# Half of the row sums of w_ada moved off TensorE, and another opening

## The chip, the cores and the metric

The kernel runs on one core of a Trainium2 chip. The metric is the time of one execution in microseconds (us) as the device reports it. A profiled execution gives, for every instruction, when it began and ended on its engine. The engines are TensorE (PE in the profile; PEld is its weight load), VectorE (DVE), ScalarE (ACT), GpSimd (POOL) and SyncE (SP, which here only issues DMAs). SBUF is the memory on the chip that all of them read, PSUM the one into which TensorE writes its products.

## What is computed

One decoder layer for a sequence of 1024 tokens, width 2048, in float32:

```python
mod = silu(c) @ W_ada + b_ada            # c: (1, 2048), W_ada: (2048, 6144)
shift, scale, gate = split(mod, 3)
h = rms_norm(x, norm_gain) * (1 + scale) + shift
proj = h @ w_in                          # w_in: (2048, 8192)
...                                      # stick-breaking attention and chunkwise retention
x = x + gate * (concat(oa, ob) @ w_out)
```

The case is about the first line. `silu(c) @ W_ada` is the product of one row with a matrix: every row j of W_ada is multiplied with one number of silu(c), and all rows are added. The text calls this the row sums.

## The kernel before

Float32 operands are cut into a high and a low part (`hi`, `lo`), and one product is three passes on TensorE: hi hi, hi lo, lo hi (`mm3`). SBUF tiles of 128x512 come from a common stock of slots (`get`, `put`); every tile of a load holds its slot until `put`.

The first 220 us or so are the starter. It multiplies seven heads' columns of w_in with the first half of the tokens (hf 0), then with the second half (hf 1). Each half is a loop over p = 0 to 15, one p for each 128 rows of the contraction, in the order KCS1 or KCS. In each p a loop runs over seven heads, `start_mm` making three products of 128x512 for each. Between the heads stand the preparations for later p: `x_turn` transposes a block of x on TensorE into a PSUM bank, `make_h` makes the normalized h_hi (ScalarE) and h_lo (VectorE), and `cut_w` cuts the weights into wh (ScalarE) and wl (VectorE). In the second half also `pieces()` stands there, which makes the factors of the later main loop, some steps on ScalarE and some on VectorE, and SP stores them.

The modulation is made in this starter, too. W_ada's columns come in chunks of 256, chunk `cc` as eight tiles of 128 partitions, each with two rows j of W_ada side by side, from SP (`load_ada`). `ada_sums(cc)` adds the rows on TensorE: sixteen products with `silu_z` as weights, which give 32 rows each, in four column groups of the array; the result `accp` lies in the PSUM bank with the tag C, of which there is one, and is copied to SBUF by VectorE. `ada_mod(cc)` transposes it (`mod`, again bank C) and reduces it on VectorE. `x_turn` writes to bank C as well, so that the three follow each other in it: whoever writes next waits until the one before has been read. Chunks 2 to 8 are made in the first half (scale), 9 to 15 in the second (shift). The very first 128-column blocks (0 to 3) are summed by `first_sums` and `first_mod` out of `ada_first` tiles.

The opening: nothing can be multiplied until x's first block (`x_first`) is transposed, `first_sums(0)` has given the modulation, h_hi is made and w_in's first tiles (`wr`) are cut. `rows` collects norm_gain, b_ada and three small gains by five small loads; they are transposed (`rows_ps`) and copied to `cols`, from which `scale_b1` and the gain come that `first_mod` needs. `keep_on(n)` issues n transposes of the identity that nobody reads, to keep TensorE busy.

TensorE's order is written by hand throughout (`manual_schedule`). ScalarE and VectorE are written by hand for p < 6 (WRITTEN) and again from the second half on; between the two, and for SP and GpSimd until the second half, a scheduler sets the order. Each engine then works strictly in its order, and waits at an instruction whose inputs aren't there.

## Time and profile before

| what | value |
|---|---|
| median of 3 runs | 1836.8 us (1835.78 to 1839.69) |
| profiled execution | 1837.35 us, its span in the profile 1835.6 us |
| TensorE busy | 1825.9 us, 99% of the span |
| VectorE busy | 1387.3 us, 76% |
| ScalarE busy | 874.0 us, 48% |
| GpSimd busy | 85.2 us, 5% |
| granted TensorE clock | 1.0 |
| DMA | 541.00 MB, mean 295 GB/s |

A row of a timeline begins with its start from the span's start and its length in us, then engine, line of the kernel, operation, output and inputs, shapes, count, and in brackets how long the engine was idle before it and what ended that. A group's row has instructions and count, busy us, mean ns of one, and the idle time before them by what ended it.

### The profile page before, as it was taken

The page shows a single profiled execution, that of the slowest core. Times are in us where ns is not written, and L with a number is a line of the kernel's source. Part 1 is how long each engine was busy: PE and PEld are TensorE (multiplying, and loading weights), DVE is VectorE, ACT ScalarE, POOL GpSimd, SP SyncE. Part 2 cuts the span into 40 slices and gives each one's busy share as a digit, 9 for nine tenths or more (in the row PEclk, how much of TensorE's full clock was granted, in tenths as well). Part 3 has the DMA queues.
Part 4 walks back from the last instruction along what each step waited for, and adds up shares of the span by engine and source line. Part 5 has one row for each costly group of instructions (what it writes and reads, how often), then busy time and mean ns, then how long its engine had stood idle before and what let it go on. Part 6 is the DMA issues. An engine that isn't in the chain of part 4 may idle for free.

```text
span 1835.6 us, 28397 instructions
## 1 busy us (share of the span) xinstructions
PE 1825.9 (99%) x9284; PEld 1504.0 (82%) x9284; DVE 1387.3 (76%) x2653; ACT 874.0 (48%) x1659; POOL 85.2 (5%) x222
## 2 busy tenths in 40 slices
PE   9999999999999999999999999999999999999999
PEld 6777788888888888888888888888888888888887
DVE  3578876656878777877778687988798777687697
ACT  3647852234554455435544554445545566452231
POOL 0000000000100010000010101000000001000000
PEclk9999999999999999999999999999999999999999
DMA  9998999999799799978997999989998864995694
GB/s 290 355 362 266 327 354 372 368 342 310 230 312 309 248 297 307 316 266 292 304 326 265 305 294 296 313 278 310 342 335 276 299 213 147 368 346 165 216 307 160
DMA packets 441112, 541.00 MB, mean 295 GB/s; under 512 B 33658, under 2 KB 246020, under 8 KB 440964
## 3 DMA queue, kind: packets, MB, share of 16 engines
q1 hardware_dynamic: 440148, 538.78, 88.5%
q8 instruction: 73, 1.20, 0.3%
q14 instruction: 75, 0.61, 0.1%
q10 hardware_dynamic: 816, 0.40, 0.1%
HBM read 448.83 MB, written 90.22 MB: 294 GB/s over the span
## 4 chain that ended last, share of the span: by engine, by line
PE 51%; DVE 1%; ACT 0%; issue 0%; DVEq 0%
PE pj L202 9%; PE pj L204 9%; PE pj L203 9%; PE y L202 5%; PE y L204 5%; PE y L203 5%; PE sp L1573 1%; PE op L1592 1%; PE op L1594 1%; PE up L1555 1%; PE tp_B L1362 0%; PE oT L204 0%; PE oT L203 0%; PE oT L202 0%; PE zp L202 0%; PE zp L204 0%
## 5 line engine op out<-in xcount | busy, mean ns | idle before, releaser
L191 DVE TENSOR_TENSOR wl<-A,wh 128x512 fp32r<-128x512 f32 x392 | 270.5, 691 | 186.4 <-ACT wh L189 175.2
L189 ACT ACTIVATE wh<-A 128x512 fp32r<-128x512 f32 x392 | 247.1, 631 | 337.2 <-PE pj L203 316.1
L413 ACT ACTIVATE c<-pj 128x512 f32<-128x512 f32 x112 | 66.5, 599 | 120.7 <-PE pj L204 119.3
L312 DVE TENSOR_TENSOR A<-A,A 128x512 f32<-128x512 f32 x160 | 108.7, 685 | 1.7
L1326 ACT ACTIVATE om<-zp,y 128x128 f32<-128x128 f32 (+2 forms) x96 | 55.7, 580 | 103.6 <-PE zp L204 63.5
L417 DVE TENSOR_TENSOR c<-pj,c 128x512 f32<-128x512 f32 x104 | 69.7, 686 | 38.8 <-PE pj L204 38.6
L202 PE MATMUL first<-h_hi,wh_first 128*128 128x512 f32 x224 | 94.9, 424 | 0.2 <-ACT h_hi L648 0.2
L1342 DVE TENSOR_TENSOR_SCAN om<-om 128x128 f32<-128x128 f32 (+2 forms) x96 | 93.6, 975 | 1.1
L202 PE MATMUL pj<-T1h,wh 128*128 128x512 f32 x232 | 94.1, 405 | 0.0
L202 PE MATMUL pj<-B22h,wh 128*128 128x512 f32 x232 | 92.7, 400 | 0.0
L202 PE MATMUL pj<-B21h,wh 128*128 128x512 f32 x232 | 92.5, 399 | 0.0
L202 PE MATMUL pj<-B11h,wh 128*128 128x512 f32 x232 | 91.2, 393 | 0.0
L204 PE MATMUL pj<-T1h,wl 128*128 128x512 f32 x232 | 90.6, 391 | 0.0
L203 PE MATMUL pj<-T1l,wh 128*128 128x512 f32 x232 | 90.6, 390 | 0.0
L203 PE MATMUL pj<-B21l,wh 128*128 128x512 f32 x232 | 90.6, 390 | 0.0
L204 PE MATMUL pj<-B22h,wl 128*128 128x512 f32 x232 | 90.6, 390 | 0.0
L204 PE MATMUL pj<-B21h,wl 128*128 128x512 f32 x232 | 90.6, 390 | 0.0
L203 PE MATMUL pj<-B22l,wh 128*128 128x512 f32 x232 | 90.4, 390 | 0.0
L203 PE MATMUL pj<-B11l,wh 128*128 128x512 f32 x232 | 90.4, 390 | 0.0
L204 PE MATMUL pj<-B11h,wl 128*128 128x512 f32 x232 | 90.4, 389 | 0.0
L202 PE MATMUL pj<-T3h,wh 128*128 128x512 f32 x224 | 89.7, 401 | 0.0
L202 PE MATMUL pj<-T4h,wh 128*128 128x512 f32 x224 | 89.7, 400 | 0.0
(425 smaller groups left out, 4975.3 us busy)
## 6 DMA issues: line engine op xcount, KB each, us to landing
A<-in_w_in_dram SPq DMA_DIRECT2D x228, 256.0 KB, 5.7
ada<-in_w_ada_dram SPq DMA_DIRECT2D x112, 256.0 KB, 5.5
wB<-in_w_out_dram SPq DMA_DIRECT2D x112, 256.0 KB, 5.6
gr<-in_w_ada_dram SPq DMA_DIRECT2D x64, 256.0 KB, 5.6
T2h<-fac_T SPq DMA_DIRECT2D x56, 256.0 KB, 5.2
T2l<-fac_T SPq DMA_DIRECT2D x56, 256.0 KB, 5.6
T1h<-fac_T SPq DMA_DIRECT2D x56, 256.0 KB, 5.3
T1l<-fac_T SPq DMA_DIRECT2D x56, 256.0 KB, 5.5
```

Source lines behind the costliest of these rows:

```text
L189: nc.scalar.activation(hi[:, 0:n], src[:, 0:n], AF.Copy)
L191: nc.vector.tensor_tensor(lo[:, 0:n], src[:, 0:n], hi[:, 0:n].bitcast(F32), op=ALU.subtract)
L202: nc.tensor.matmul(o, a_hi, b_hi, start=first, stop=False, skip_group_check=on)
L203: nc.tensor.matmul(o, a_hi, b_lo, start=False, stop=False, skip_group_check=on)
L204: nc.tensor.matmul(o, a_lo, b_hi, start=False, stop=last, skip_group_check=on)
L312: nc.vector.tensor_tensor(r[o], r[a], r[b], op=ALU.add if n == 1 else ALU.subtract)
L413: nc.scalar.activation(order(t), o, AF.Copy)
L417: nc.vector.tensor_tensor(t, o, t, op=ALU.add)
L1326: nc.scalar.activation(om[:, :n], zp[:, :n], AF.Sigmoid, scale=y[:, 16 + i:17 + i])
L1342: nc.vector.tensor_tensor_scan(rev, rev, rev, init, op0=ALU.mult, op1=ALU.bypass)
L1555: nc.tensor.matmul(up[:, j * P:(j + 1) * P], kd[:, j * P:(j + 1) * P], vb(4 * g + j), start=True, stop=True)
L1573: nc.tensor.matmul(sp[:, j, :], r["k", g][:, tk], r["q", g][:, tk], start=True, stop=True)
```

## The change

For the eleven chunks of `APART` (4 to 7 and 9 to 15; chunks 2, 3 and 8 stay) TensorE adds only rows j = 8 to 15. Rows 0 to 7 are added elsewhere:

- chunks 4 to 7 (first half): VectorE adds rows 0 to 3 (`row_sums`, one multiply and three multiply-adds of 128x256), GpSimd multiplies and adds rows 4 to 7 (`beside`: two multiplies and one addition of 128x512, one addition of 128x256);
- chunks 9 to 15 (second half): ScalarE multiplies each of the eight rows in place (`scaled`, eight times 128x256), GpSimd adds them (`beside`: three additions of 128x512, one of 128x256).

VectorE adds these parts where it copied `accp` before (`ada_added`; two additions for chunks 4 to 7, one for the others). The sum now has no empty rows, so the reduction in `ada_mod` runs over all 128 numbers of each of the two blocks, where it read one in 32. In the first half, the sums stand one head later, and the transposes `mod` of it one head later, too.

In the opening the fillers are single-pass products of a float32r copy of the identity, 32, 7 and 14 of them instead of 8, 4 and 6 transposes, and 5 and 3 more stand between the first three products. The fourth `ada_first` tile is loaded from ScalarE's queue, ahead of `x_first`. VectorE's and ScalarE's hand-written order begins earlier. x's second quarter (qt 1) for the first four blocks is loaded in halves at p = 4, and the blocks 4, 5 and 6 of x are loaded one p later, the statistics of blocks 4 and 5 too.

```diff
-XQ_LOAD = {4: 1, 8: 3}
+XQ_LOAD = {8: 3}
-X_LOAD = {5: (4,), 7: (5,), 9: (6,), 11: (7,)}
-X_STAT = {8: (4,), 10: (5,), 12: (6,), 13: (7,)}
+X_LOAD = {6: (4,), 8: (5,), 10: (6,), 11: (7,)}
+X_STAT = {9: (4,), 11: (5,), 12: (6,), 13: (7,)}
+APART = (4, 5, 6, 7, 9, 10, 11, 12, 13, 14, 15)
...
+    ident_r = cons.tile([P, P], F32R, name="ident_r")
+    written = ExitStack()
+    written.enter_context(tc.manual_schedule(engines={mybir.EngineType.Activation, mybir.EngineType.DVE}))
+    nc.vector.tensor_copy(ident_r, ident)
...
+    nc.scalar.dma_start(ada[0, 0, 3].rearrange("p (j n) -> p j n", n=P), ada_rows[:, 12:16, D:D + P])
+    nc.scalar.dma_start(x_first.rearrange("p (t n) -> p t n", n=P), x2[0:HALF, 0:P].rearrange("(t p) n -> p t n", p=P))
...
-    def mm3(o, a_hi, a_lo, b_hi, b_lo, first, last, on=False):
+    def mm3(o, a_hi, a_lo, b_hi, b_lo, first, last, on=False, between=None):
         nc.tensor.matmul(o, a_hi, b_hi, start=first, stop=False, skip_group_check=on)
+        if between:
+            between(5)
         nc.tensor.matmul(o, a_hi, b_lo, start=False, stop=False, skip_group_check=on)
+        if between:
+            between(3)
...
+    def scaled(cc, g):
+        for j in (2 * g, 2 * g + 1):
+            src = ada[cc, g][:, (j % 2) * 2 * P:(j % 2 + 1) * 2 * P]
+            nc.scalar.activation(src, src, AF.Copy, scale=silu_c[:, j:j + 1])
+
+    def beside(cc):
+        t = [ada[cc, g] for g in range(4)]
+        if cc < 8:
+            for g in (2, 3):
+                nc.gpsimd.tensor_tensor(by_two(t[g]), by_two(t[g]), pair(g), op=ALU.mult)
+            nc.gpsimd.tensor_tensor(t[2], t[2], t[3], op=ALU.add)
+            nc.gpsimd.tensor_tensor(t[2][:, 0:2 * P], t[2][:, 0:2 * P], t[2][:, 2 * P:HALF], op=ALU.add)
+            return
+        for a, b in ((0, 1), (2, 3), (2, 0)):
+            nc.gpsimd.tensor_tensor(t[a], t[a], t[b], op=ALU.add)
+        nc.gpsimd.tensor_tensor(t[2][:, 0:2 * P], t[2][:, 0:2 * P], t[2][:, 2 * P:HALF], op=ALU.add)
+
+    def row_sums(cc, j):
+        src, acc = ada[cc, j // 2][:, (j % 2) * 2 * P:(j % 2 + 1) * 2 * P], ada[cc, 0][:, 0:2 * P]
+        if j == 0:
+            nc.vector.tensor_scalar(acc, src, silu_c[:, 0:1], None, op0=ALU.mult)
+        else:
+            nc.vector.scalar_tensor_tensor(acc, src, silu_c[:, j:j + 1], acc, op0=ALU.mult, op1=ALU.add)
+
     def ada_sums(cc):
+        j0 = 8 if cc in APART else 0
...
-        for j in range(16):
+        for j in range(j0, 16):
...
+    def ada_added(cc, ap_):
         acc = get(f"acc_{cc}")
-        nc.vector.tensor_copy(acc[:, 0:256], ap_)
+        if cc not in APART:
+            nc.vector.tensor_copy(acc[:, 0:256], ap_)
+            return acc
+        t = [ada.pop((cc, g)) for g in range(4)]
+        if cc < 8:
+            nc.vector.tensor_tensor(acc[:, 0:256], ap_, t[0][:, 0:256], op=ALU.add)
+            nc.vector.tensor_tensor(acc[:, 0:256], acc[:, 0:256], t[2][:, 0:256], op=ALU.add)
+        else:
+            nc.vector.tensor_tensor(acc[:, 0:256], ap_, t[2][:, 0:256], op=ALU.add)
+        put(*t)
         return acc
...
-                nc.tensor.transpose(idle, ident, ident)
+                nc.tensor.matmul(idle, ident_r, ident_r, start=True, stop=True)
-        keep_on(8)
+        keep_on(32)
         x_turn(0, 0, "pj", 4)
-        keep_on(4)
+        keep_on(7)
...
-        keep_on(6)
+        keep_on(14)
...
+            if p % 2 and h == 2 and c + 2 in APART and c + 2 < 8:
+                beside(c + 2)
+            if p % 2 == 0 and h < 4 and c + 1 in APART:
+                if p == WRITTEN and h == 0:
+                    beside(c + 1)
+                row_sums(c + 1, h)
-            if p % 2 == 0 and h == 3:
+            if p % 2 == 0 and h == 4:
                 sums[c + 1] = ada_sums(c + 1)
             if p % 2 and p < KC - 1 and h == 0:
+                sums[c + 1] = ada_added(c + 1, sums[c + 1])
+            if p % 2 and p < KC - 1 and h == 1:
                 ada_mod(c + 1, sums.pop(c + 1))
...
+            if p % 2 == 0 and cc < 15 and 2 <= i < 6:
+                scaled(cc + 1, i - 2)
+            if p % 2 == 0 and cc < 15 and i == 6:
+                beside(cc + 1)
             if i == 4 and p % 2 and cc < 15:
-                sums[cc + 1] = ada_sums(cc + 1)
+                sums[cc + 1] = ada_added(cc + 1, ada_sums(cc + 1))
```

Three places of the built program, engine by engine. First SP in the opening, before: the tiles are the fourth block of W_ada's first 128 columns, the five parts of `rows`, w_in's first two tiles and the rest of x's first block. The waits in brackets named DMAHW are for the load that used the same of eight semaphores before.

```order
L818 DMA ada_first_2_301<-in_w_ada_dram 128x4x128
L818 DMA ada_first_3_303<-in_w_ada_dram 128x4x128
L850 DMA rows<-in_norm_gain_dram 16x128 [waits DVE_49]
L851 DMA rows<-in_b_ada_dram 32x128
L852 DMA rows<-in_sb_q_gain_dram 1x128 [waits DMAHW0_49]
L853 DMA rows<-in_sb_k_gain_dram 1x128 [waits DMAHW1_49]
L854 DMA rows<-in_ret_norm_gain_dram 8x128 [waits DMAHW2_49]
L752 DMA wr_0_0_310<-in_w_in_dram 128x512 [waits DMAHW3_49]
L752 DMA wr_0_1_312<-in_w_in_dram 128x384 [waits DMAHW4_49]
L889 DMA x_0_274<-in_x_dram 128x384 [waits DMAHW5_49]
```

And after, on the same engine:

```order
L945 DMA x_0_277<-in_x_dram 128x384 [waits DMAHW0_49]
L945 DMA x_0_278<-in_x_dram 128x384 [waits DMAHW1_49]
L945 DMA x_0_279<-in_x_dram 128x384 [waits DMAHW2_49]
L945 DMA x_0_280<-in_x_dram 128x384 [waits DMAHW3_49]
L876 DMA ada_first_0_425<-in_w_ada_dram 128x4x128 [waits DMAHW4_49]
L876 DMA ada_first_1_427<-in_w_ada_dram 128x4x128 [waits DMAHW5_49]
L876 DMA ada_first_2_429<-in_w_ada_dram 128x4x128 [waits DMAHW6_49]
L906 DMA rows<-in_norm_gain_dram 16x128 [waits DMAHW7_49,DVE_49]
L907 DMA rows<-in_b_ada_dram 32x128 [waits DMAHW0_49]
L908 DMA rows<-in_sb_q_gain_dram 1x128 [waits DMAHW1_49]
L909 DMA rows<-in_sb_k_gain_dram 1x128 [waits DMAHW2_49]
L910 DMA rows<-in_ret_norm_gain_dram 8x128 [waits DMAHW3_49]
```

The loads of `rows`, fifth to ninth on SP before, now stand thirteenth to seventeenth, behind w_in's tiles, x's and three tiles of the second block of W_ada.

Second, ScalarE in the second half, between h_hi of one p and the weights' cut for p + 2; T2h and T4h are pieces of the factors. Before:

```order
L648 ACTIVATE h_hi_1_2303<-xT_1_2282,mods 128x512
L658 ACTIVATE T2h_2316<-T_1_2245 128x512
L189 ACTIVATE wh_first_1_0_2325<-wr_1_0_2258 128x512
L658 ACTIVATE T4h_2332<-xT_0_773 128x512
L189 ACTIVATE wh_first_1_1_2337<-wr_1_1_2260 128x384
```

After (the eight scalings, each row standing for one or two of them):

```order
L706 ACTIVATE h_hi_1_2368<-xT_1_2347,mods 128x512
L631 ACTIVATE ada_0_2153<-ada_0_2153,silu_c 128x256 x2
L631 ACTIVATE ada_1_2155<-ada_1_2155,silu_c 128x256 x2
L716 ACTIVATE T2h_2385<-T_1_2310 128x512
L631 ACTIVATE ada_2_2157<-ada_2_2157,silu_c 128x256 x2
L198 ACTIVATE wh_first_1_0_2396<-wr_1_0_2323 128x512
L631 ACTIVATE ada_3_2159<-ada_3_2159,silu_c 128x256 x2
L716 ACTIVATE T4h_2405<-xT_0_822 128x512
L198 ACTIVATE wh_first_1_1_2414<-wr_1_1_2325 128x384
```

Eight scalings now stand ahead of and between the cuts, in every second p.

Third, TensorE in the first half, where bank C goes from `mod` to the transposes of x (`xtp`). Before:

```order
L630 MATMUL mod_1194<-ident,acc_1156 128x128 x2
L202 MATMUL first_0_424<-h_hi_0_1161,wh_first_0_0_1000 128x512
L203 MATMUL first_0_424<-h_lo_0_1163,wh_first_0_0_1000 128x512
L204 MATMUL first_0_424<-h_hi_0_1161,wl_first_0_0_1002 128x512
L202 MATMUL first_0_435<-h_hi_0_1161,wh_first_0_0_1000 128x512
L203 MATMUL first_0_435<-h_lo_0_1163,wh_first_0_0_1000 128x512
L204 MATMUL first_0_435<-h_hi_0_1161,wl_first_0_0_1002 128x512
L597 MATMUL xtp_0_1208<-ident,x_1_762 128x128
```

And after:

```order
L687 MATMUL mod_1240<-ident,acc_1234 128x128 x2
L211 MATMUL first_0_480<-h_hi_0_1180,wh_first_0_0_1047 128x512
L214 MATMUL first_0_480<-h_lo_0_1182,wh_first_0_0_1047 128x512
L217 MATMUL first_0_480<-h_hi_0_1180,wl_first_0_0_1049 128x512
L609 MATMUL xtp_0_1251<-ident,x_1_787 128x128
```

Between the two now stands one head (three products), where there were two: `mod` has moved one head later, and the transposes of x have stayed.

More of the change, by code (lines that the diff above doesn't have):

```diff
@@ L533, in layer_kernel @@
     nc.vector.memset(qb, 0.0)
-    ada, xT = {}, {}
+    xT = {}
     def load_x(t):
@@ L632, in ada_mod @@
         mod = sm.tile([P, 2], F32, tag="mod", name=f"mod_s_{cc}")
-        nc.vector.tensor_reduce(mod, turned.rearrange("p (s g r) -> p s g r", s=2, r=32)[:, :, :, 0],
-                                mybir.AxisListType.X, ALU.add)
+        view = (turned.rearrange("p (s g r) -> p s g r", s=2, r=32)[:, :, :, 0] if cc not in APART
+                else turned.rearrange("p (s r) -> p s r", s=2))
+        nc.vector.tensor_reduce(mod, view, mybir.AxisListType.X, ALU.add)
         k0 = 2 * (CHUNKS1[cc] if cc < 8 else CHUNKS[cc - 8])
@@ L774, in start_mm @@
             sl = slice(h % 4 * P, (h % 4 + 1) * P)
-            mm3(first[h], hi[:, sl], lo[:, sl], h_hi[kc, hf], h_lo[kc, hf], p == 0, p == KC - 1)
+            mm3(first[h], hi[:, sl], lo[:, sl], h_hi[kc, hf], h_lo[kc, hf], p == 0, p == KC - 1, between=between)
     def load_xq(qt):
@@ L844, in first_mod @@
         nc.vector.tensor_tensor(mods[:, s:s + 1], mods[:, s:s + 1], gain_c[:, s:s + 1], op=ALU.mult)
-    written = ExitStack()
-    written.enter_context(tc.manual_schedule(engines={mybir.EngineType.Activation, mybir.EngineType.DVE}))
     with tc.high_priority(AHEAD):
-        load_first(0)
+        load_first(0, (0, 1, 2))
         nc.sync.dma_start(rows[0:16, 0:P], norm_gain.rearrange("o (k p) -> (o k) p", p=P))
@@ L896, in loads @@
     def loads(p):
-        if p == 2:
-            load_xh(2, 0)
+        if p in (2, 4):
+            load_xh(2 if p == 2 else 1, 0)
         if p < WRITTEN:
```

32 lines of the change are left out of this document (21 added, 11 removed).

## The prediction

> **What bounds the kernel now.** I read the page's busy shares first, then busy time in stretches that run from one row-sum block to the next, then the timelines of the engines that the change loads.
>
> ```profile
> PE 1825.9 (99%) x9284; PEld 1504.0 (82%) x9284; DVE 1387.3 (76%) x2653; ACT 874.0 (48%) x1659; POOL 85.2 (5%) x222
> ```
>
> TensorE is busy 99% of the span, so work taken from it shortens the run as long as nobody else becomes late. The next view tells how much room the others have where the change works. Columns: stretch, length, then busy us of PE, PEld, DVE, ACT and POOL, granted clock, DMA share, GB/s. Each stretch begins at the start of a chunk's row sums; chunks 4 to 7 are made in the first four, chunk 8 (untouched) in the stretch 99.49:112.79 left out here, chunks 9 to 15 in the last seven.
>
> ```profile
> 50.03:60.66 10.63, 10.08 (x70) 6.90 (x70) 4.79 (x11) 5.44 (x14) 0.00 (x0) 1.00 1.05 353
> 60.66:73.49 12.83, 12.83 (x86) 9.70 (x85) 8.14 (x27) 11.15 (x28) 0.00 (x0) 1.00 1.06 353
> 73.49:86.67 13.18, 13.05 (x85) 9.67 (x84) 7.42 (x27) 9.16 (x23) 0.00 (x0) 1.00 1.05 357
> 86.67:99.49 12.82, 12.82 (x86) 9.71 (x85) 10.19 (x55) 8.19 (x18) 0.00 (x0) 1.00 1.05 363
> ...
> 112.79:131.51 18.72, 18.72 (x114) 14.60 (x113) 13.04 (x24) 8.03 (x14) 0.00 (x0) 1.00 1.06 362
> 131.51:144.32 12.81, 12.81 (x85) 9.69 (x84) 9.32 (x18) 7.31 (x13) 0.00 (x0) 1.00 1.02 335
> 144.32:157.13 12.81, 12.81 (x85) 9.69 (x84) 11.86 (x22) 10.00 (x19) 0.00 (x0) 1.00 0.36 126
> 157.13:169.95 12.82, 12.82 (x86) 9.70 (x85) 11.22 (x22) 9.87 (x18) 0.00 (x0) 1.00 0.99 321
> 169.95:182.76 12.81, 12.81 (x85) 9.69 (x84) 9.81 (x19) 9.74 (x18) 0.00 (x0) 1.00 0.98 322
> 182.76:195.57 12.81, 12.81 (x85) 9.70 (x84) 10.16 (x19) 9.93 (x18) 0.00 (x0) 1.00 1.03 343
> 195.57:208.39 12.82, 12.82 (x86) 9.70 (x85) 10.00 (x19) 9.73 (x18) 0.00 (x0) 1.00 1.05 333
> ```
>
> TensorE fills each stretch, but VectorE already needs 9.3 to 11.9 of 12.8 us in the second half and ScalarE about 9.8. GpSimd does nothing there.
>
> **Taken from TensorE.** A chunk's row sums, the first product behind them, and the next writer of the same PSUM bank C, the transposes of x:
>
> ```profile
> 157.13 1.93 PE L616 MATMUL accp<-ada,silu_z 128*32 128x256 f32 x32
> 159.00 0.50 PE L202 MATMUL first<-h_hi,wh_first 128*128 128x512 f32 x1
> ...
> 161.17 0.60 PE L597 MATMUL xtp<-ident,x 128*128 128x128 f32 x4
> ```
>
> Sixteen products (32 passes) take 159.00 - 157.13 = 1.87 us. Half of that is 0.93 us, and eleven chunks give 10.2 us. The bank is written again 161.17 - 159.00 = 2.2 us after the sums end, and VectorE must have emptied it by then: VectorE may be about 2 us late, no more, before TensorE stands still.
>
> **Given to the others.** The durations:
>
> ```profile
> L1579 POOL TENSOR_TENSOR rq<-rq,dm x16: 1291/1300/1569, 1204.3 to 1510.1; 128x512 f32<-128x512 f32 x16
> L1121 DVE SCALAR_TENSOR_TENSOR ga<-gr,silu_c,ga 128x256 f32<-128x256 f32 x97 | 47.0, 484 | 1.8
> L620 DVE COPY acc<-accp 128x256 f32<-128x256 f32 x14 | 5.9, 425 | 19.2 <-PE accp L616 19.2
> L633 DVE TENSOR_REDUCE mod_s<-mod 128x2 f32<-128x8 f32 x13 | 2.1, 161 | 1.5 <-PE mod L630 1.3
> L648 ACT ACTIVATE h_hi<-xT,mods 128x512 fp32r<-128x512 f32 x16 | 11.4, 715 | 0.2
> L189 ACT ACTIVATE wh_first<-wr 128x512 fp32r<-128x512 f32 x16 | 10.0, 624 | 10.7 <-DMA wr<-in_w_in_dram 6.5 <-PE accp L616 3.1 <-PE first L203 1.0
> L189 ACT ACTIVATE wh_first<-wr 128x384 fp32r<-128x384 f32 x16 | 8.4, 522 | 14.5 <-PE first L203 14.4
> ```
>
> GpSimd: three operations of 1.30 us and one of half the size, an estimated 0.67, so 4.6 us a chunk. VectorE, chunks 4 to 7: three multiply-adds of 0.48, one multiply (estimate 0.24), a second addition (0.42, as the copy), and a reduction over 256 numbers where it had 8 (0.42 as the copy, for 0.16, so 0.26 more): 2.4 us. Chunks 9 to 15: only the 0.26, taken as 0.3, since the addition stands where the copy stood. ScalarE, chunks 9 to 15: eight scalings of 256 columns. A scaling of 512 takes 0.715; 128 columns less take 0.10 (0.624 to 0.522), so 256 take 0.51, and with the overlap of neighbours some 0.42: 3.4 us a chunk.
>
> **What these cost each other.** VectorE beside GpSimd, at three places of the trace:
>
> ```profile
> 1204.28 1.57 POOL L1579 TENSOR_TENSOR rq<-rq,dm 128x512 f32<-128x512 f32 x1 [51.32 <-PE sp L1573]
> 1204.02 0.68 DVE L312 TENSOR_TENSOR A<-A,A 128x512 f32<-128x512 f32 x1
> 1204.62 1.78 DVE L191 TENSOR_TENSOR wl<-A,wh 128x512 fp32r<-128x512 f32 x1
> ...
> 1517.52 1.47 POOL L487 TENSOR_TENSOR c<-u,c 128x512 f32<-128x512 f32 x1 [1.43 <-ACT u L483]
> 1517.77 1.77 DVE L1801 TENSOR_TENSOR A11o<-A11o,A21o 128x512 f32<-128x512 f32 x1
> ...
> 1243.74 1.30 POOL L1579 TENSOR_TENSOR rq<-rq,dm 128x512 f32<-128x512 f32 x1 [28.20 <-DVE st L1602]
> 1244.46 0.66 DVE L1578 TENSOR_TENSOR pT<-sp,dm 128x512 f32<-128x512 f32 x1
> ```
>
> A VectorE operation with two SBUF inputs that meets a GpSimd one takes 1.78 or 1.77 us for 0.68: it ends 0.55 us after GpSimd's (1204.28 + 1.57 = 1205.85; 1204.62 + 1.78 = 1206.40), so it stood still until GpSimd was done. With one input in PSUM (1244.46) it loses nothing. VectorE's work in these stages (h_lo, wl, the pieces of the factors, the multiply-adds) nearly all has two SBUF inputs. The trace holds no four such GpSimd operations in a row, so I bound the loss per chunk: 0 if they fall on idle time, 4.6 us if VectorE stands all that time; at 1.09 us for each 1.30 it is 3.8, and as VectorE is busy some 8 tenths of the time, I take 3.0.
>
> The Trainium skill's page "SBUF — State Buffer", section "Who interferes with whom", says the same more strictly: the later of the two waits for the whole instruction. Read as a full 4.6 us a chunk, that rule would add 9 x 1.6 = 14 us to the sum below, near 1857 us; the rows are milder, and I keep them.
>
> VectorE against TensorE's new stretch (old one less 0.93), in order. Chunk 4: 4.79 + 5.4 fits with what was idle around it. Chunk 5: 8.14 + 5.4 - 11.9 = 1.6 us too much; 6: 7.42 + 5.4 - 12.25 = 0.6; 7: 10.19 + 5.4 - 11.89 = 3.7. Chunk 9 fits (13.04 + 3.3 of 17.8). Chunk 10: 9.32 + 3.3 - 11.88 = 0.7; 11: 3.3; 12: 2.6; 13: 1.2; 14: 1.6; 15: 1.4. Together 16.7 us, of which 2 us in each of the two halves vanish in VectorE's allowed lateness: 12.7 us of waiting for TensorE. What is late next is bank C: the addition that empties it now also waits for GpSimd's last addition, and the cuts wl and h_lo queue behind it on VectorE. In the first half the transposes of x follow `mod` after one head instead of two, which leaves that reduction less time; I count this inside the 2 us.
>
> ScalarE alone would be over, too: 10.00 + 3.4 - 11.88 = 1.5 us for chunk 11, then 1.4, 1.3, 1.4 and 1.2, in sum 6.8. It is a floor under the second half that runs at the same time as VectorE's excess, so it is not added.
>
> Sums part: -10.2 + 12.7 = +2.5 us.
>
> **The opening.**
>
> ```profile
> 2.00:6.50 4.50, 2.55 (x13) 2.15 (x12) 0.35 (x2) 1.26 (x2) 1.00 (x4) 1.00 1.07 288
> 9.12 0.48 PE L873 MATMUL rows_ps<-ident,rows 128*128 128x128 f32 x1
> 11.78 0.80 PE L202 MATMUL first<-h_hi,wh_first 128*128 128x512 f32 x1 [0.21 <-ACT h_hi L648]
> 14.19 0.63 PE L203 MATMUL first<-h_lo,wh_first 128*128 128x512 f32 x1
> 14.62 0.63 PE L204 MATMUL first<-h_hi,wl_first 128*128 128x512 f32 x1
> ...
> 18.56 0.40 PE L203 MATMUL first<-h_lo,wh_first 128*128 128x512 f32 x1
> 18.80 0.40 PE L204 MATMUL first<-h_hi,wl_first 128*128 128x512 f32 x1
> PE xtp L597 <- DMA x<-in_x_dram: 0.5, 2, 0.3
> ```
>
> The five small loads into `rows` were SP's fifth to ninth; now twelve larger ones stand ahead of them. Nothing on TensorE passes `rows_ps` before they land, and the first modulation, h_hi and the first product need it. Ahead of them lie, by their shapes, seven pieces of w_ada and x_first (256 KB each, 2.1 MB), w_in's 448 KB and x's 768 KB: 3.3 MB. At 288 GB/s from 2 us on that is 11.5 us, so `rows` lands near 13.5 instead of before 9.12. From `rows_ps` to the first product took 2.66 us, 0.4 of it ScalarE's lateness behind late w_in; the first product then starts near 15.8 instead of 11.78, 4.0 us later. Against it: products stood 0.43 us apart at 14.2 and 0.24 at 18.6; at the faster pace the nine before 17.2 would end up to 1.7 us sooner, of which I credit 1.0, and 0.5 for the two waits for x that are gone. Opening: +2.5 us, bounds -0.5 (small loads pass the large ones) and +4.5. The 32 fillers, the 8 between products and the halved loads of x cost nothing by themselves: the fillers run while TensorE waits for x_first, `rows`, or h_lo (0.2 us if not), and the loads behind others in a queue that never empties.
>
> The Trainium skill's page "TensorE: Matmul & The Clock Gate", Part 1 and Part 4, says that about 3.4 us of real products bring full speed, that transposes do not count, and that as long an idle time ends it. By that rule the fillers would have saved the whole 1.7 us if `rows` came early; here the idle time before `rows_ps` lets it fall again. The profile's clock column reads 1.00 in the opening, so only the spacing shows it.
>
> **Sum.** +2.5 + 2.5 = +5.0 us on the profiled execution's 1837.35 (span 1835.6; the median of the runs is 0.55 lower, 1836.8): 1842 us.
>
> **Rivals.** First, the sums stay hidden: VectorE loses under 1 us a chunk, because GpSimd's operations meet idle time or PSUM reads. Then only chunks 7, 11 and 12 are over, by less than the lateness allowed, and the time is 1837.35 - 10.2 + 2.5 = 1829.6. For it speaks that VectorE idles 1 to 3.5 us a stretch; against it, that the in-order idle times are waits that it needs. This rival ends on the other side, and it decides from a loss under 2.4 us a chunk, where the whole sum is zero. Second, ScalarE binds and VectorE follows: 6.8 - 2 us of waiting, -10.2 + 4.8 + 2.5, 1834.5 us, not told from no change. Third, GpSimd takes 3.8 us a chunk from VectorE: 9 x 0.8 more, 1849.5.
>
> **How the numbers follow.** Forecast 0.43, the third rival 0.12, the first 0.22, the second 0.18, and 0.05 for an early `rows` together with the forecast's sums (1839). The 0.2% is 3.7 us: faster is below 1833, slower above 1840.5. So faster 0.22; same 0.18 + 0.05 and 0.02 of the forecast's lower part, 0.25; slower 0.41 + 0.12, 0.53. The range, 1830 to 1851, reaches from the hidden case to GpSimd's stronger hold; the forecast's own is 1838 to 1847.
>
> **What would show it.** After the change: `rows_ps` and the first product near 13.5 and 15.8; L616 blocks of about 0.95 us; VectorE operations of 1.1 to 1.8 us beside GpSimd's; waits of TensorE for VectorE at the transposes of x, and stretches of 12.5 to 15 us for chunks 11 to 15. Stretches of 11.9 us there would prove the forecast wrong, as would `rows_ps` near 9.

## The result, and the profile after

The changed kernel takes 1866.4 us (median of 4 runs, 1864.5 to 1868.2) where the kernel before takes 1836.4 us in the same comparison: 1.016 times as long, 95% interval 1.0142 to 1.0177. The forecast was 1842 us with a range of 1830 to 1851. The direction was right, the size was not: 30 us instead of 5. One execution among all that are reported here, of 10484.1 us, belongs to the last kernel under "VectorE alone" and enters no ratio.

All numbers of the profile below are of one execution with a span of 1866.5 us, 30.9 more than before. First the page's busy line, then TensorE's waits (who waited for whom, us in all, times, longest). Before, the same view held 5.6 us in all, 3.4 of it in the first 6 us of the run.

```profile
PE 1833.5 (98%) x9151; PEld 1511.1 (81%) x9151; DVE 1423.9 (76%) x2674; ACT 893.9 (48%) x1715; POOL 141.8 (8%) x266
```

```profile
PE xtp L609 <- DVE acc L676: 8.1, 6, 2.7
PE accp L660 <- ACT xT L615: 4.2, 4, 1.6
PE first L214 <- DVE h_lo L708: 4.0, 1, 4.0
PE pj L217 <- DVE wl L200: 2.3, 1, 2.3
PE xtp L609 <- DVE mod_s L692: 2.2, 3, 1.1
...
PE mod L687 <- ACT xT L615: 1.4, 1, 1.4
PE rows_ps L929 <- DMA rows<-in_b_ada_dram: 1.2, 1, 1.2
PE first L217 <- DVE wl_first L200: 0.9, 1, 0.9
PE mod L687 <- DVE acc L669: 0.8, 1, 0.8
```

TensorE has fewer row sums to make but is busy 7.6 us longer, and behind the opening it has 23.9 us of new waits (8.1, 4.2, 4.0, 2.3, 2.2, 1.4, 0.9, 0.8), where the starter before had 0.55. The stretches from one row-sum block to the next show where; the columns are those of the prediction. The first begins with chunk 2's sums, the five behind the dots with those of chunks 10 to 14.

```profile
43.59:65.30 21.71, 16.73 (x89) 12.14 (x88) 10.12 (x16) 6.67 (x15) 6.62 (x6) 0.84 1.07 352
...
160.50:175.20 14.70, 12.41 (x68) 9.03 (x68) 14.02 (x22) 12.61 (x26) 5.58 (x5) 1.00 0.21 79
175.20:191.63 16.43, 13.73 (x68) 10.37 (x68) 15.54 (x23) 13.31 (x27) 6.01 (x5) 0.90 0.79 258
191.63:206.24 14.61, 12.62 (x69) 8.95 (x69) 12.85 (x19) 12.03 (x26) 4.37 (x5) 1.00 0.88 291
206.24:219.68 13.44, 12.19 (x68) 9.10 (x68) 12.96 (x20) 13.05 (x26) 5.58 (x5) 1.00 0.93 294
219.68:235.63 15.95, 12.51 (x69) 9.03 (x69) 12.18 (x18) 12.66 (x26) 5.59 (x5) 1.00 0.98 296
```

Before, the stretch behind chunk 2 was this one:

```profile
36.19:50.03 13.84, 13.74 (x89) 10.03 (x88) 5.34 (x11) 6.67 (x15) 0.00 (x0) 1.00 0.99 326
```

It took 13.84 us, and those behind chunks 10 to 14 took 12.8 us each. Now the first takes 21.71, and the five of the second half 13.4 to 16.4, with VectorE busy 12.2 to 15.5 us of each. The lag of the start of a block behind the same block before gives a sum that leaves nothing out:

| part of the run | lag at its end | added | forecast |
|---|---|---|---|
| opening, to chunk 2 | 7.4 | +7.4 | +2.5 |
| chunk 2 to chunk 3 | 15.3 | +7.9 | 0 |
| chunk 3 to chunk 8 (rest of the first half) | 15.2 | -0.1 | +0.2 |
| chunk 8 to the first product of the main loop | 26.5 | +11.3 | +2.3 |
| main loop and end | 30.9 | +4.4 | 0 |

Such lags, here and below, are read from one profiled execution of each kernel. In the eleven traces that have the opening of before, chunk 2's sums begin within 1.1 us of each other, so a lag of less than that tells little.

The granted clock is the other new thing. Stretches of 2.5 us, same columns; the third number from the right is the clock:

```profile
52.50:55.00 2.50, 0.50 (x1) 0.19 (x1) 2.50 (x3) 0.00 (x0) 2.38 (x2) 0.98 1.07 355
55.00:57.50 2.50, 1.77 (x6) 1.59 (x7) 2.31 (x3) 0.00 (x0) 2.34 (x3) 0.50 1.09 360
...
182.50:185.00 2.50, 2.50 (x8) 1.94 (x7) 2.50 (x5) 2.50 (x6) 0.00 (x0) 0.58 1.00 325
...
297.50:300.00 2.50, 2.50 (x6) 2.02 (x7) 1.88 (x3) 2.50 (x6) 0.00 (x0) 0.50 1.05 304
```

Behind TensorE's three longest waits (4.03 us at 54, 2.70 at 181, 2.29 at 297) the clock stands at 0.50, for 6.8, 3.4 and 3.4 us, read in steps of half a microsecond. At half the clock that loses, by estimate, half of 13.6, 6.8 us, so that a wait of 2.7 us costs 4.4. The parts add up to 7.4 for the opening, 23.9 of waits, 6.8 of slow clock, less what TensorE was spared (a block of sums to the next product takes 161.50 - 160.50 = 1.00 us where it took 1.87: 0.87 x 11 = 9.6), 28.5 of the 30.9 us.

### The profile page after: what moved, and what is told of

Its sections match the earlier page's. It is cut to its first block, busy times and chain, and to the rows that moved or that the text cites. A ratio compares the mean times of both kernels' runs of the same rounds, so it can differ in the third digit from the quotient of the medians.

```text
span 1866.5 us, 28312 instructions
## 1 busy us (share of the span) xinstructions
PE 1833.5 (98%) x9151; PEld 1511.1 (81%) x9151; DVE 1423.9 (76%) x2674; ACT 893.9 (48%) x1715; POOL 141.8 (8%) x266
## 4 chain that ended last, share of the span: by engine, by line
PE 50%; DVE 1%; ACT 0%; issue 0%; DVEq 0%
PE pj L211 9%; PE pj L217 9%; PE pj L214 9%; PE y L211 5%; PE y L214 5%; PE y L217 5%; PE sp L1645 1%; PE op L1664 1%; PE op L1666 1%; PE up L1627 1%; PE tp_B L1434 0%; PE oT L217 0%; PE oT L214 0%; PE oT L211 0%; PE zp L211 0%; PE zp L214 0%
## 5 line engine op out<-in xcount | busy, mean ns | idle before, releaser
L1401 POOL TENSOR_SCALAR_AFFINE_SELECT om<-om 128x128 f32<-128x128 f32 x64 | 29.2, 456 | 884.1 <-ACT om L1398 796.7
L214 PE MATMUL first<-h_lo,wh_first 128*128 128x512 f32 x224 | 89.8, 401 | 4.0 <-DVE h_lo L708 4.0
L217 PE MATMUL first<-h_hi,wl_first 128*128 128x512 f32 x224 | 90.0, 402 | 0.9 <-DVE wl_first L200 0.9
L217 PE MATMUL pj<-T3h,wl 128*128 128x512 f32 x224 | 88.3, 394 | 2.3 <-DVE wl L200 2.3
```

The lines of the kernel that those rows point to most:

```text
L214: nc.tensor.matmul(o, a_hi, b_lo, start=False, stop=False, skip_group_check=on)
L217: nc.tensor.matmul(o, a_lo, b_hi, start=False, stop=last, skip_group_check=on)
L1401: nc.gpsimd.affine_select(om[:, n - P:n], om[:, n - P:n], pattern=[[-1, P]], compare_op=ALU.is_gt, fill=1.0, base=0, channel_multiplier=1)
```

## Experiments

### Which part costs what

The changed kernel with no chunk split (the opening, the loads of x and the later sums of the first half stay):

```diff
-APART = (4, 5, 6, 7, 9, 10, 11, 12, 13, 14, 15)
+APART = ()
```

> The changed kernel with no chunk split: every chunk is summed by TensorE as before, and what stays is the opening (fillers, order of the first loads), the loads of x at other places, and the sums of the first half one head later. Theory (late rows and fillers on the path): the whole lateness of the opening, 7.4 us by the lag of chunk 2 between the two traces, and nothing more, so 1844 us against 1836.4, and no stall of TensorE near 50 us. Rival one (the new loads of x near p = 4 delay chunk 4's tiles for everybody): 15 us, 1852. Rival two (the opening's lateness is made up later): 1838.

Measured: 1863.9 us, 1.0152 (1.0135 to 1.0168). The second half's scalings and GpSimd additions do not look at APART. They were still issued, on tiles that TensorE then summed in full, so only the run up to chunk 8 is the opening alone, and the total says nothing on the three theories. Up to there the lag is 7.1 us at chunk 2 and 7.2 at chunk 8, with no stall near 50 us: the opening costs its 7 us, and they are neither made up nor added to. In the second half TensorE then waited 11.4 us for GpSimd's additions into the tiles it was about to sum.

The other way round, the opening and x's loads of before with the sums of after (the diff of front's opening and of X_LOAD, X_STAT and XQ_LOAD, reversed):

> The changed kernel with the opening and the loads of x as before: only the split sums stay. In this program VectorE's row sums of chunk 4 stand behind the h_lo and the cuts of two p, not ahead of them. Theory (the stall near 50 us is one of place in VectorE's order): 1866.4 less 7.4 for the opening and less 7.9 for chunk 4's place, 1851 us. Rival one (chunk 4's stall comes from work that is too much wherever it stands, or from GpSimd's hold on VectorE): 1859. Rival two (the sums as I predicted them, +2.5): 1839.

Measured: 1856.3 us, 1.0105 (1.009 to 1.012), 5 more than the theory and 17 more than my sum. The lag is -0.8 at chunk 4, +4.0 at chunk 8, +14.9 at the first product of the main loop, +16.1 fifty us on. The stall of 7.9 us that chunk 4's work caused is gone, as the theory said, but the rest of the first half now costs 4.8 us. Nor is the place in VectorE's order shown to be what removed the stall, since chunk 4's tiles are loaded sooner here, too. SP issues them from 42.39 us on; before the change and in the changed kernel it was this:

```profile
43.21 5.27 SPq L546 DMA_DIRECT2D ada<-in_w_ada_dram  x8
...
42.15 2.42 SPq L884 DMA_DIRECT2D x<-in_x_dram  x4
...
46.72 4.20 SPq L558 DMA_DIRECT2D ada<-in_w_ada_dram  x8
```

The four loads of x that the change put at p = 4 stand ahead of chunk 4's, which are issued 3.5 us later than before.

Chunk 4 alone back on TensorE:

```diff
-APART = (4, 5, 6, 7, 9, 10, 11, 12, 13, 14, 15)
+APART = (5, 6, 7, 9, 10, 11, 12, 13, 14, 15)
```

> The changed kernel with chunk 4 summed by TensorE alone again; ten chunks stay split. Theory: the wait for h_lo (4.0 us), the one for wl (0.95) and the half clock behind them (about 3.3 us) go, TensorE gets 0.93 us of work back: 1866.4 - 7.9 + 0.9, 1859 us. Rival (chunk 5's row sums, which wait for their loads in the same way, take over the stall): 1866 or more. If the half clock does not depend on the wait, only 4 us go: 1862.

Measured: 1863.4 us, 1.0144 (1.0129 to 1.0159). The rival was right on what happens, though not on its number (1866 or more): lags of 6.9 at chunk 3, 11.1 at chunk 4 and 15.4 at chunk 5. Chunk 5's row sums wait 4.35 us for their load, ahead of the copy of chunk 3's sums. Ahead of the reduction of chunk 4's stand, among other work, two row sums of chunk 6 (0.83 us). Of this kernel's waits of TensorE:

```profile
PE mod L687 <- DVE acc L669: 2.9, 1, 2.9
PE xtp L609 <- DVE mod_s L692: 2.5, 1, 2.5
```

Each of the two is followed by 3.4 us at half clock. Fewer fillers behind the first modulation:

```diff
-        keep_on(14)
+        keep_on(4)
...
-            start_mm(p, 0, w, (h,), keep_on if p == h == 0 else None)
+            start_mm(p, 0, w, (h,))
```

> The changed kernel with 4 fillers ahead of the first product where it had 14, and none between the first three products. With this, VectorE's row sums of chunk 4 also come to stand behind h_lo and the cuts of the next p. Theory: fillers behind the first modulation lie on the path (first product 1.2 us sooner, the first three products 1.1 us closer), and chunk 4's stall of 7.9 us goes: 1856 us. Rival one (only the fillers' 2.3 us go, since the stall is chunk 4's lateness): 1864. Rival two (the fillers raise the clock, as they would if they counted as work): the products stay 0.43 us apart for longer, and the time is 1858 to 1868.

Measured: 1858.6 us, 1.0117 (1.01 to 1.0134). The first product starts at 17.25 us instead of 18.30, and chunk 2 comes 1.6 us sooner, so the fillers do lie on the path; as with them, the products stay 0.43 us apart until about 23 us. From chunk 2 to chunk 4 the lag still grows by 6.2 us (in the profiled execution, the slowest of four, 4.7 us above their median): row sums that stand later on VectorE stall it too, in four waits for h_lo and wl of 1.2, 1.2, 1.2 and 0.6 us. VectorE waits 2.07 us for chunk 4's load here, and the h_lo and the two cuts behind its row sums take 4.3 us for 1.9 beside GpSimd. Place alone is not the cause; how much of the stall is the late load's and how much GpSimd's, no run tells.

### The second half: ScalarE or GpSimd?

The opening and x's loads as before, chunks 9 to 15 split, 4 to 7 not:

> The opening and the loads of x as before, chunks 9 to 15 split, chunks 4 to 7 by TensorE alone: only the second half of the change. In four kernels so far TensorE fell 10.9 to 11.3 us behind in the second half, whatever came ahead of it. Theory (that cost is the second half's own): 1836.8 + 11, 1848 us. Rival (it depends on the lateness that the first half leaves behind): 1840 or less.

Measured: 1852.1 us, 1.0078 (1.0062 to 1.0093). The lag is 1.1 at chunk 8 (the sums one head later), 11.5 at the first product of the main loop, 14.1 fifty us on. The second half's 10.4 us are its own, whatever comes before. The time is 4 us over the theory's 1848, by the 1.1 ahead of it and 2.6 in the main loop behind it.

The same without GpSimd's additions, and the same without ScalarE's scalings:

```diff
-            if p % 2 == 0 and cc + 1 in APART and i == 6:
-                beside(cc + 1)
```

> As the one with the second half alone, but GpSimd's four additions per chunk are left out (so rows 0 to 3, 6 and 7 are missing from the sums of chunks 9 to 15); ScalarE's eight scalings and VectorE's addition stay. Theory L (GpSimd holds VectorE up by some 2.8 us a chunk, and that makes VectorE late): VectorE is back at before plus 0.3 us a chunk and the time falls by 8 us or more, to 1832 to 1840. Theory A (ScalarE's scalings stand ahead of the copies and cuts that TensorE waits for, and ScalarE is 3.4 us a chunk fuller): the time stays within 3 us of the kernel with the second half alone, 1845 or more.

```diff
-            if p % 2 == 0 and cc + 1 in APART and 2 <= i < 6:
-                scaled(cc + 1, i - 2)
```

> As the one with the second half alone, but ScalarE's eight scalings per chunk are left out (so rows 0 to 7 are added unscaled); GpSimd's four additions stay. Theory L (GpSimd's hold on VectorE): 1845 us or more. Theory A (ScalarE's place and load): 1832 to 1840. If both are needed for the loss, each of the two kernels gains most of the 11 us.

Measured: without the additions 1841.3 us, 1.0021 (1.0011 to 1.003); without the scalings 1850.4 us, 1.0067 (1.0052 to 1.0082). The second half adds 2.1 us in the first (lag 1.3 to 3.4) and 12.9 in the second (0.4 to 13.3). GpSimd's additions decide. Taking the scalings away while GpSimd adds brings nothing up to the main loop (12.9 us for 10.4); the total is 1.7 us lower, since the main loop then adds nothing. The stretches behind the sums of chunks 10, 11 and 12, of the kernel with the second half alone:

```profile
146.31:161.01 14.70, 12.41 (x69) 9.03 (x69) 14.02 (x22) 12.62 (x26) 5.58 (x5) 1.00 0.22 80
161.01:177.47 16.46, 13.77 (x69) 10.18 (x69) 15.95 (x23) 13.74 (x27) 6.85 (x5) 0.90 0.78 257
177.47:191.39 13.92, 12.23 (x70) 9.03 (x69) 12.65 (x19) 11.54 (x25) 4.18 (x4) 1.00 0.90 297
```

and without the additions:

```profile
144.20:157.31 13.11, 12.43 (x69) 9.03 (x69) 11.80 (x22) 12.61 (x26) 0.00 (x0) 1.00 0.25 93
157.31:171.03 13.72, 12.44 (x68) 9.02 (x68) 12.34 (x23) 12.61 (x26) 0.00 (x0) 1.00 0.93 307
171.03:184.55 13.52, 12.27 (x68) 9.10 (x68) 10.68 (x19) 12.61 (x26) 0.00 (x0) 1.00 0.96 312
```

VectorE does the same operations in both and needs 2.0 to 3.6 us more per stretch beside GpSimd. The whole second half, from chunk 8's sums to the main loop, first with additions and scalings, then without the additions, then without the scalings:

```profile
113.85:233.08 119.23, 105.90 (x585) 79.04 (x584) 103.32 (x154) 93.77 (x183) 38.93 (x28) 0.99 0.81 265
...
114.08:224.92 110.84, 104.27 (x585) 78.18 (x585) 86.62 (x156) 94.78 (x185) 0.00 (x0) 1.00 0.88 289
...
113.19:234.89 121.70, 107.81 (x584) 80.37 (x584) 108.36 (x157) 73.91 (x129) 35.74 (x26) 0.97 0.82 270
```

VectorE (the third busy time) needs 16.7 us more with the additions, 2.4 a chunk. In none of these kernels does it sit idle for a result of GpSimd's, so the loss lies in operations that are held up while they run. Without the additions TensorE still doesn't get its 11.9 us: ScalarE, 12.6 of 13.1 to 13.7 us busy, is late with the copies out of bank C (waits of 0.2 to 1.8 us for xT). The two losses do not add up. TensorE is spared 6.1 us (7 x 0.87), so the scalings alone lose 8.2 us, the additions alone 19.0, and both together 16.5. Without the scalings GpSimd starts as its loads land, and VectorE is held up longer, 21.7 us or 3.1 a chunk, so this kernel does not show what ScalarE's load costs beside an unchanged GpSimd.

What of GpSimd's work holds VectorE up? The same kernel with copies for additions:

```diff
-            nc.gpsimd.tensor_tensor(t[a], t[a], t[b], op=ALU.add)
+            nc.gpsimd.tensor_copy(t[a], t[b])
```

> As the kernel with the second half alone, but GpSimd's four additions per chunk are copies of the same shape (one input in SBUF instead of two; rows 0 to 5 are then missing from the sums of chunks 9 to 15). Theory (GpSimd holds VectorE up for the length of its operation whatever it does in SBUF): near 1852 us, in proportion to the copies' length. Rival (the hold needs two inputs on GpSimd's side): VectorE's operations beside the copies take their 0.68 us, and the time is near 1841, as without additions.

Measured: 1844.3 us, 1.0039 (1.0025 to 1.0053), between the two: 3.6 us for the second half (lag 1.35 to 4.98). A copy of 128x512 takes 0.82 us on the mean where an addition took 1.50, and VectorE's busy time over the seven chunks grows by 3.9 us instead of 16.7, with GpSimd busy 22.0 us instead of 38.9. So one input is enough to hold VectorE up, but the hold falls much faster than GpSimd's busy time. Neither theory had that.

### The first half: whose work is it?

The opening as before, chunks 4 to 7 split, additions at once and mod at the first head of the next p:

```diff
-                sums[c + 1] = ada_sums(c + 1)
+                sums[c + 1] = ada_added(c + 1, ada_sums(c + 1))
             if p % 2 and p < KC - 1 and h == 0:
-                sums[c + 1] = ada_added(c + 1, sums[c + 1])
-            if p % 2 and p < KC - 1 and h == 1:
                 ada_mod(c + 1, sums.pop(c + 1))
```

> The opening and the loads of x as before, chunks 4 to 7 split and 9 to 15 by TensorE alone; VectorE's additions follow the sums at once, and the transposes mod stand at the first head of the next p, as before the change, so that again two heads lie between mod and the transposes of x. With the late mod, the first half of the split alone put TensorE 4.7 us behind (chunk 3 to chunk 8). Theory (the one head less makes the transposes of x wait for the reduction, 2.2 + 1.3 + 1.6 us): that is gone, and the first half costs nothing: 1836.5 us. Rival one (VectorE is late wherever mod stands): 1839 to 1842. Rival two (the additions, now earlier, wait for GpSimd and hold up the cuts): 1843 or more.

Measured: 1842.8 us, 1.003 (1.0019 to 1.004). The place of mod was not it: from chunk 3 to chunk 9 the lag grows by 5.7 us (-0.8 to +4.9), where it grew by 4.8 up to chunk 8 with the later mod. Then the same without GpSimd's part, and without VectorE's four row sums:

```diff
-                beside(c + 2)
...
-                    beside(c + 1)
```

> As the kernel with the first half's sums alone and mod early, but GpSimd's four operations per chunk are left out (rows 5 and 7 of each chunk are missing from its sum, rows 4 and 6 stand there unscaled through one tile); VectorE's own part stays. That kernel fell 5.7 us behind between chunk 3 and chunk 8. Theory L (GpSimd's hold on VectorE, about 1.3 us a chunk by VectorE's busy time, and VectorE's addition that waits for GpSimd's last one): most of the loss goes, 1834 to 1838. Theory V (VectorE's own row sums stand in its order ahead of what TensorE waits for): 1840 to 1843.

```diff
-                row_sums(c + 1, h)
```

> As the kernel with the first half's sums alone and mod early, but VectorE's four row sums per chunk are left out (row 0 stands in the sum unscaled, rows 1 to 3 are missing); GpSimd's part and both additions stay. Theory V: most of the loss goes, 1834 to 1838. Theory L: 1840 to 1843.

Measured: without GpSimd 1836.7 us, 1.0001 (0.9992 to 1.001), the lag goes from -0.9 to -1.7 over the same chunks (0.8 of the 3.5 us that TensorE is spared); without VectorE's rows 1842.1 us, 1.0029 (1.0017 to 1.0041), -0.7 to +4.6. It is GpSimd again. VectorE's busy time over the four chunks is 45.4 us in the kernel with both and 35.7 without GpSimd, 2.4 us a chunk once more. Why so little held time costs so much shows at one place of the kernel with both. GpSimd, then VectorE:

```profile
90.78 2.49 POOL L632 TENSOR_TENSOR ada<-ada,silu_c 128x512 f32<-128x512 f32 x2 [9.90 <-DMA ada<-in_w_ada_dram]
93.34 1.46 POOL L633 TENSOR_TENSOR ada<-ada,ada 128x512 f32<-128x512 f32 x1
...
90.86 2.82 DVE L194 TENSOR_TENSOR wl_first<-wr,wh_first 128x512 fp32r<-128x512 f32 x2 [0.84 <-ACT wh_first L192]
93.61 0.41 DVE L667 TENSOR_TENSOR acc<-accp,ada 128x256 f32<-128x256 f32 x1
94.12 0.97 DVE L668 TENSOR_TENSOR acc<-acc,ada 128x256 f32<-128x256 f32 x1
```

The two cuts take 2.82 us for 1.15, the addition out of PSUM its 0.41, and the second addition, with both inputs in SBUF, 0.97. TensorE then waits 1.53 us at mod for that addition, and 1.48 us for the reduction behind it. The stretch has 13.65 us of VectorE in 15.58: it is not full, but the held operations are those that TensorE waits for.

### VectorE alone

Rows 0 to 3 of chunks 4 to 7 on VectorE, 4 to 15 on TensorE, nothing on GpSimd:

```diff
-        j0 = 8 if cc in APART else 0
+        j0 = 4 if cc in APART else 0
```

> Opening, loads of x and second half as before; chunks 4 to 7 with rows 0 to 3 on VectorE alone (one multiply, three multiply-adds, one addition in place of the copy), rows 4 to 15 on TensorE, nothing on GpSimd. TensorE is spared 4 x 0.47 = 1.9 us. Theory L: VectorE has room for 1.7 us a chunk without GpSimd's hold, so the time is 1835 us, just under before. Theory V: what stands ahead of h_lo and the cuts costs more than is spared, 1838 to 1841.

Measured: 1836.9 us, 1.0001 (0.9992 to 1.001); the profiled execution is 1.2 us shorter than that before, the median is not, and neither theory's time came. Rows 0 to 3 of chunks 9, 10, 13, 14 and 15 added to it (and chunk 4 left out), with fillers of the new kind:

```diff
+            if cc + 1 in APART and (i >= 5 if p % 2 == 0 else i < 2):
+                row_sums(cc + 1, i - 5 if p % 2 == 0 else i + 2)
```

> Opening's loads and order as before, but the fillers are single-pass products of the float32r identity, 16, 4 and 7 in place of 8, 4 and 6 transposes, which take about as long; chunks 5, 6 and 7 have rows 0 to 3 on VectorE alone, nothing on GpSimd or ScalarE. In the kernel with early rows the products stood 0.23 us apart from the first one on, after 53 such fillers without a pause; before, 0.43 apart until 17 us. Theory one (these products raise the clock where transposes do not): the first products 0.23 us apart, 1.7 us saved, and 1.4 by the rows on VectorE: 1833.5 us. Theory two (the pause of some 2 us before x_first lands undoes it, or the kind of filler does not matter): 1.4 us alone, 1835.

> The one before with rows 0 to 3 of chunks 9, 10, 13, 14 and 15 on VectorE alone, too (1.7 us more a chunk on VectorE, of 12.8; nothing on ScalarE and GpSimd): 5 x 0.47 = 2.3 us less on TensorE. Theory L (it was GpSimd's hold and ScalarE's load that made bank C late, not VectorE's own work): 2.3 us less than the one before, 1831 to 1833. Theory V (VectorE, busy 9.3 to 11.4 of 12.8 us there, is late as soon as anything is added): slower than the one before by 1 us or more.

Measured: first half and fillers 1837.8 us, 1.0005 (0.9996 to 1.0014); both halves 1836.2 us, 0.9998 (0.9989 to 1.0007). The fillers, whose identity came late on VectorE, began at 4.58 us and made chunk 2 2.6 us late, so the question on the clock was not answered. The second half with VectorE alone gains: its lag goes from 0.0 at chunk 8 to -1.7, against +0.9 to +0.3 in the kernel without it. With the old opening, and with fillers that begin at 1.69 us:

> The opening exactly as before (transposes as fillers, old order of loads), rows 0 to 3 of chunks 4 to 7, 9, 10, 13, 14 and 15 on VectorE alone, rows 4 to 15 on TensorE; nothing on GpSimd, nothing more on ScalarE. TensorE is spared 9 x 0.47 = 4.2 us. In the two runs with parts of it, 1.2 us of the first half's 1.9 and about 1.0 us of the second half's 2.3 came out. Theory (these add up): 1836.8 - 2.2, 1834.6 us, 0.9988 of before. If all 4.2 us came out: 1832.6. Rival (VectorE late in one of the two makes up for it): 1836 or more.

> As that one without chunk 4, and with the fillers as 16, 4 and 7 single-pass products that begin near 1.7 us (in the run with new fillers they began at 4.6 us, since the copy of the identity stood late on VectorE, and lay on the path). The loads keep their old order. Theory one (these products count for the clock where transposes do not, also across a wait of up to 2 us for x_first): the first products 0.23 us apart, chunk 2 begins 1.5 us sooner than before. Theory two (the kind of filler does not matter, the clock comes up some 6 us after the first long products): chunk 2 within 0.5 us of before, as in the one before.

Measured: 1836.5 us, 0.9997 (0.9988 to 1.0005), and 1835.4 us, 0.9992 (0.9983 to 1.0001). In the profiled execution of the first the lag is -2.8 us at the main loop, so VectorE's own rows pay where GpSimd is silent, but the medians cannot tell any of the five kernels of this part from the one before, and the sum of gains that was expected (1834.6 us) did not come. None beats it by a measurable amount. The early fillers do not pay either: TensorE's short instructions run faster from 8.6 us on, then h_hi and h_lo come late by 0.74 and 0.29 us, the products stand 0.43 us apart again from 12 to 15 us, and chunk 2 comes 0.3 us sooner than before. In its trace four waits for x of 0.2 to 0.4 us near 57 us are followed by 3.4 us at half clock, and the lag grows by 3.1 us from chunk 3 to chunk 4.

### The opening

Why is it 7 us late? Of the changed kernel, SP and TensorE:

```profile
3.57 2.96 SPq L945 DMA_DIRECT2D x<-in_x_dram  x4
9.09 1.48 SPq L876 DMA_DIRECT2D ada_first<-in_w_ada_dram  x3
10.69 0.42 SPq L906 DMA_DIRECT2D rows<-in_norm_gain_dram  x1
...
1.69 7.09 PE L922 MATMUL idle<-ident_r 128*128 128x128 f32 x32 [1.69 <-DVE ident_r L149]
9.21 1.08 PE L609 MATMUL xtp<-ident,x_first 128*128 128x128 f32 x4 [0.43 <-DMA x_first<-in_x_dram]
...
14.76 0.45 PE L929 MATMUL rows_ps<-ident,rows 128*128 128x128 f32 x1 [1.21 <-DMA rows<-in_b_ada_dram]
15.28 3.23 PE L922 MATMUL idle<-ident_r 128*128 128x128 f32 x14
18.30 0.73 PE L211 MATMUL first<-h_hi,wh_first 128*128 128x512 f32 x1
```

SP stood from 6.53 to 9.09 us, since each of its next loads waits for the one eight places before it, and issued rows only at 10.69. Before:

```profile
2.97 0.50 SPq L850 DMA_DIRECT2D rows<-in_norm_gain_dram  x1
```

Also x_first lands near 9.2 us instead of 5.4. And the 14 fillers end after h_hi, which ScalarE finished at 17.06. The test puts the loads of rows back, in a kernel with the new opening alone:

```diff
-    nc.vector.tensor_copy(ident_r, ident)
...
     nc.vector.memset(rows[:, 0:P], 0.0)
+    nc.vector.tensor_copy(ident_r, ident)
```

> The new opening alone (no chunk split, no scalings, no GpSimd additions), with the copy of the identity one instruction later on VectorE, so that the five loads of rows stand fourth to eighth on SP again; fillers, the load of the fourth piece from ScalarE's queue and x's loads are those of the change. Theory one (the late rows are the whole 7.2 us): 1838. Theory two (behind rows stand x_first, which lands near 9.1 us instead of 5.4, and 21 fillers of 0.22 us between it and the first product): the first product starts near 17 us instead of 18.2, and the time is 1842 to 1843.5. If the fillers bring the clock up once rows is early: products 0.23 us apart from the first on, 1836 to 1840.

Measured: 1847.1 us, 1.0055 (1.0041 to 1.0069). Its opening:

```profile
1.69 7.09 PE L922 MATMUL idle<-ident_r 128*128 128x128 f32 x32 [1.69 <-DVE ident_r L163]
8.57 1.07 PE L609 MATMUL xtp<-ident,x_first 128*128 128x128 f32 x4
...
13.41 1.76 PE L922 MATMUL idle<-ident_r 128*128 128x128 f32 x14
15.01 0.45 PE L211 MATMUL first<-h_hi,wh_first 128*128 128x512 f32 x1
...
16.65 0.39 PE L211 MATMUL first<-h_hi,wh_first 128*128 128x512 f32 x1
16.88 0.40 PE L214 MATMUL first<-h_lo,wh_first 128*128 128x512 f32 x1
```

The first product starts at 15.01 us, the second head's products are 0.23 us apart, and chunk 2 is only 1.5 us late, 5.9 us less than 7.4. Of these, 3.3 are there at the first product, by the place of five small loads. The rest is the faster pace behind it, and the loads are not shown to bring that: with one and the same opening of before, in eleven traces, the pace rises anywhere between 8.7 and 17.4 us. x_first lands here at 7.2 us, by GpSimd's wait for it, so that the 32 fillers, until 8.57, lie on the path. The total is higher for another reason. With block 4 of x loaded one p later, ScalarE now has its squares ahead of the cuts, and waits 7.28 us for that load; TensorE then waits 7.2 us at mod. With the late rows, in the first run with the opening alone, ScalarE waits for x 1.2 us at most.

## Why the prediction failed, step by step

**Bound and saving.** Right: TensorE bound the kernel, and was spared 0.87 us a chunk (0.93 forecast).

**Durations given to the others.** Mostly right, where nothing held them up: eight scalings 3.5 us (3.4), multiply-adds 0.48, the reduction 0.41 (0.42); the first multiply took 0.35 (0.24). GpSimd's four operations take 4.6 us a chunk in the first half, as forecast, and 5.6 in the second, since its additions take 1.50 us there.

**GpSimd's hold, 3.0 us a chunk.** 2.4 in each half alone, 3.1 in the second without the scalings. The Trainium skill's page "SBUF — State Buffer", section "Who interferes with whom", has the later of the two wait for the whole of the other's operation. The trace shows this where they meet (2.82 us for 1.15), and a chunk's total stays at 2.4 us beside 4.6 and 5.6 of GpSimd's. That VectorE does not always have such an operation ready is the likely reason, not a shown one.

**From held time to TensorE's waiting.** This step failed. I compared VectorE's busy time with the length of a stretch, and called what fits free. By that rule 2.4 us a chunk is the point where my first rival breaks even; measured at that very price were +11.3 us in the second half and +5.7 in the first half alone. VectorE works in order, and the held operations (h_lo, wl, the addition that empties bank C) are those for which TensorE waits next. In the sum, 12.7 us of TensorE's waiting were forecast; measured were 23.9, and 6.8 of slow clock behind them. The 2 us of lateness that I allowed each half are not to be seen: even without GpSimd's additions, with ScalarE's load, TensorE waited 6.5 us in the second half, in waits of 0.2 to 1.8. That the rest of the first half came out near the forecast (-0.1 for +0.2) is luck: with the sums alone it cost 4.8 us.

**ScalarE's floor, "not added".** Not refuted. Alone, the scalings lost 8.2 us where the floor was 6.8; beside GpSimd's additions, taking them away gained nothing up to the main loop.

**Chunk 4 "fits with what was idle".** Wrong by 7.9 us. Its own sum was 0.5 us over (4.79 + 5.4 against 9.7), and the work did not fall into that stretch but into the one before, which the prediction did not price. The order of the program shows it: VectorE's row sums of chunk 4 stand ahead of h_lo and the cuts of p = 4. VectorE in the changed kernel:

```profile
50.87 0.35 DVE L650 TENSOR_SCALAR ada<-ada,silu_c 128x256 f32<-128x256 f32 x1 [3.63 <-DMA ada<-in_w_ada_dram]
...
52.70 1.53 DVE L708 SCALAR_TENSOR_TENSOR h_lo<-xT,mods,h_hi 128x512 fp32r<-128x512 f32 x1
54.15 3.07 DVE L200 TENSOR_TENSOR wl_first<-wr,wh_first 128x512 fp32r<-128x512 f32 x2
```

3.63 us for chunk 4's load, then the row sums, then h_lo and two cuts held up by GpSimd (4.5 us for 1.9). That the moved loads of x cost nothing does not hold either: they stand ahead of chunk 4's on SP. The order of VectorE, on which the largest term stood, was not looked at.

**The opening, +2.5.** 7.4. The reason was right (rows land late, 14.7 us for 13.5), its size was not: I counted bytes, and SP's wait for its earlier loads came on top. "Fillers cost nothing" was wrong for those behind the first modulation: 1.6 us for 18 of the 22, by the run without them. The 0.5 us for two waits for x do not belong here: in the trace before, these waits stand between 57 and 59 us. The clock credit of 1.0 did not come, and not because an idle time undid it: the last of the 32 fillers was as slow as the first, so there was nothing to fall. With early rows the pace rose sooner, but one trace cannot show that the fillers did it, since with the opening of before the moment varies by 8.7 us.

**A clock that falls.** Not in the prediction outside the opening: 6.8 us.

**The main loop, 0.** 4.4 us, of which 2.29 is one wait for wl near 297 us and 1.7 the half clock behind it. VectorE stands there 5.34 us until a store of T1h is done. Before the change it stands there longer, 6.34 us, without TensorE noticing. A wait for wl of 0.7 to 2.3 us came there in all runs with ScalarE's scalings but the one with the opening alone. It did not come in the run without scalings, 13 us late, and of the runs with the old second half one had it (0.56 us). What decides it stays open.

**Rivals.** The hidden case (1829.6) fell with the step from held time to waiting; the one with ScalarE as the bound put the second half at -1.7 us (4.8 less 6.5 spared), and the run without the additions measured +2.1; the one with 3.8 us a chunk had the mechanism, and its price would still have been 17 us short.

## What to carry to other kernels

Idle time of an engine that works in order is no room: before work is put on it, read in its order which instruction stands behind the new one and who waits for that, and do the same for the loads on a queue that is moved. What two engines lose on the same path can neither be added up nor taken as the larger of the two: here 8.2 and 19.0 us alone were 16.5 together, because taking one away moved the other's work. Of TensorE's waits of 2 us or more, 12 of 16 cost more than their length, so price them with the slow clock behind them.
